# Attention scores on halves of the array's rows, norm rows loaded later, six further weight slots

## The chip, the cores and the metric

The kernel runs on one core of a Trainium2 chip. Such a core has a matrix engine (PE, TensorE), a vector engine (DVE), an activation engine (ACT), GpSimd (POOL), a queue engine (SP) that here issues the weight loads, and 16 DMA engines that all queues share. The metric is the device time of one execution in microseconds (us). 0.5% of it is 6.5 us.

## What is computed

Two layers over 256 tokens of width 1024. Layer 0 mixes by attention, layer 1 by a Hyena convolution; each is followed by a layer norm, a mixture of experts (16 experts, two per token) and a second layer norm. Only layer 0's attention and the very last layer norm are touched:

```python
def diff_attention(q, k, v, lam):            # 4 heads x 2 maps of width 64, q: 256 rows, k: 512
        s = jnp.einsum('bqhmd,bkhmd->mbhqk', q_blk, k).astype(jnp.float32) * scale
        p = jax.nn.softmax(s, axis=-1)
        a = (p[0] - lam * p[1]).astype(v.dtype)

def window_gqa_latent(q, k, v, k_ctx, v_ctx, sink):   # 8 query heads of width 64, 2 key heads
    s_loc = jnp.einsum('bnqhgd,bnkhd->bnhgqk', qb, kb).astype(jnp.float32) * scale
    s_ctx = jnp.einsum('bnqhgd,bchd->bnhgqc', qb, k_ctx).astype(jnp.float32) * scale

    for i in range(DEPTH):
        ...
        x = layer_norm(DEEPNORM_ALPHA * x + g1 * y, ln_g[i, 0], ln_b[i, 0])
        f = moe_ffn(x * (1 + sc2) + sh2, router_w, router_bias, exp_w_gate[i], exp_w_up[i], exp_w_down[i])
        x = layer_norm(DEEPNORM_ALPHA * x + g2 * f, ln_g[i, 1], ln_b[i, 1])
```

## The kernel before

**Weights.** All weights come in loads of 1 MB on SP's queue (`load`, L144), each into a slot of 8 KB per partition. There is a ring of 12 slots, and in the expert part of layer l there are MORE[l] further slots, w0, w1, ..., through which the ring then turns too (`all_slots`). A load waits until the instructions that read the slot's last content are done, and SP takes its loads strictly in order. A transfer is thus started by the engine that frees a slot, nearly always PE.

**Attention (layer 0).** `proj` makes the projections (L937), and a `fin_` function each finishes them per 128 tokens: rope on DVE, transposes on PE into a bank of PSUM, an evacuation by ACT (`evac`, L162). A head is 64 wide, the array has 128 rows. fin_q therefore writes each query head into a tile zq with a block of 64 zeros (memset by POOL) in the middle, and transposes it twice, shifted by 64, so that qaZ and qwZ hold the transposed query of one head on one half of the rows and zeros on the other. A score (diff_scores L1004, win_scores L1033) is then one matmul over all 128 rows, 128 queries by 512 keys, against both heads' keys; two of them (m = 0, 1) make a unit, each followed by its maximum on DVE (L1005, L1035). `interleave` writes units, their outputs (L1021, L1060) and the further projections and modulation vectors (DVE L269; their sums on PE, L281, in column strips of 32) among one another. A scheduler at build time sets each engine's order from that.

**Experts.** A layer has ten places p. Each place loads an expert's 12 MB (four pairs of gate and up, four down), multiplies the gathered tokens (`up` L646, `down` L665, `back` L684, DVE L690), and places 1 to 8 also carry a piece of a dense treatment of the two fullest experts: odd ones `dense_up` (L709, four loads), even ones `dense_down` (L721, two loads). At p == 9 (NEST) there are first MORE[l] loads of the tenth expert into the further slots, then the `back` of the ninth, then `rare`: a nest of conditional branches (L759) for cases that these inputs don't have, which every engine passes by itself without doing anything; and behind it the remaining 12 − MORE[l] loads into the ring and the tenth expert's work. One place earlier, `all_slots(0)` takes the further slots out of the ring.

**End.** The last layer norm's factors (gbf, 1 MB for all 128 partitions) are loaded by POOL right after the first layer's end (L1399), into a pool of their own. L359 to L365 make the statistics, L1407 and L1408 the rows, and four transfers store them.

## Time and profile before

| | us |
|---|---|
| median of three runs | 1301.54 (1300.76 to 1306.81) |
| the profiled execution | 1297.5 |
| its span, first to last instruction | 1295.7 |
| PE busy | 1161.9 (90%) |
| DVE busy | 549.3 (42%) |
| ACT busy | 214.9 (17%) |

All rows come from the profiled execution; its times count from the span's start. A row of the timeline joins instructions of one kind: start, duration, engine, line, operands, and the number of records in it. Matrix products in f32 leave two records each. A busy PE says that matmuls overlap without a gap, not how fast they are: the start of the next row tells more than the duration of one. A row of the waits names the engine and line that waited, what it waited for, the time in all, how often, and the longest. "SPq", "PEq" are the queues of SP and PE: the time in which an engine handles its branches and semaphores.

### The profile page before, as it was taken

How to read it: one execution, taken by the hardware profiler on the slowest of the kernel's cores; microseconds unless marked ns; L12 is line 12 of the kernel's file. 1: busy time of each engine (PE TensorE's matmuls, PEld its weight loads, DVE VectorE, ACT ScalarE, POOL GpSimd, SP SyncE). 2: the span in 40 equal slices, each digit the busy share in tenths (PEclk: the TensorE clock that was granted, in tenths of full speed). 3: DMA queues.
4: the chain of work that ended last, by engine and by line, in shares of the span. 5: the costliest groups of instructions: out<-in, count | busy, mean ns of one | idle time of the engine just before them, and what ended most of it. 6: DMA issues, size and time to landing. Idle time of an engine off the chain costs nothing. (4 is left out here: it accounts for less than half of the span.)

```text
span 1295.7 us, 19951 instructions
## 1 busy us (share of the span) xinstructions
PE 1161.9 (90%) x8106; PEld 696.2 (54%) x8106; DVE 549.3 (42%) x1131; ACT 214.9 (17%) x431; POOL 48.8 (4%) x88
## 2 busy tenths in 40 slices
PE   5999989979999989999686779899699999999983
PEld 2345645448437466485443468684374374665741
DVE  2376998461231432414311268993712213223133
ACT  2133646120000000000000044410300000000000
POOL 1000000210000000000200010000100000000000
PEclk9999999989999999999778789999899999999986
DMA  9999894879998998999999784378799999999964
GB/s 325 397 402 349 307 356 180 310 263 406 409 401 340 400 401 329 397 398 363 382 385 395 294 345 177 109 299 316 266 405 408 402 358 396 405 373 401 408 249 196
DMA packets 133206, 443.87 MB, mean 343 GB/s; under 512 B 8271, under 2 KB 9895, under 8 KB 133104
## 3 DMA queue, kind: packets, MB, share of 16 engines
q1 hardware_dynamic: 127168, 426.76, 85.0%
q0 software_dynamic: 4864, 13.18, 3.0%
q10 hardware_dynamic: 1072, 2.54, 0.6%
q8 instruction: 67, 1.10, 0.3%
q14 instruction: 35, 0.29, 0.1%
HBM read 437.19 MB, written 5.26 MB: 341 GB/s over the span
## 5 line engine op out<-in xcount | busy, mean ns | idle before, releaser
L646 PE MATMUL acc<-w,xe 128*32 128x256 f32 (+1 forms) x2688 | 217.6, 430 | 11.4 <-PEq L759 5.9
L709 PE MATMUL acc<-xnT,w 128*128 128x256 f32 x1024 | 222.3, 379 | 0.0
L709 PEld LDWEIGHTS acc<-xnT,w 128*128 128x128 f32 x1024 | 194.4, 190 | 25.6
L646 PEld LDWEIGHTS acc<-w,xe 128*32 128x32 f32 (+1 forms) x2688 | 102.4, 120 | 115.0 <-issue 66.6
L665 PE MATMUL acc<-w,aT 128*32 128x256 f32 (+1 forms) x1344 | 115.5, 420 | 10.2 <-DMA w<-in_exp_w_down 6.0
L721 PE MATMUL acc<-w,hid 128*128 128x512 f32 x256 | 111.4, 593 | 0.3 <-DVE xs L690 0.3
L712 DVE TENSOR_TENSOR hid<-hid,acc 128x256 f32<-128x256 f32 x32 | 13.5, 421 | 197.0 <-ACT hid L711 197.0
L665 PEld LDWEIGHTS acc<-w,aT 128*32 128x32 f32 (+1 forms) x1344 | 47.5, 116 | 63.6 <-issue 27.4
L269 DVE SCALAR_TENSOR_TENSOR w<-w,cz 128x1024 f32<-128x1024 f32 x60 | 75.8, 1289 | 11.4 <-DMA w<-in_mod_w 11.4
L721 PEld LDWEIGHTS acc<-w,hid 128*128 128x128 f32 x256 | 48.1, 190 | 58.1 <-issue 57.3
L690 DVE TENSOR_TENSOR xs<-xs,acc 128x512 f32<-128x512 f32 x92 | 57.4, 682 | 47.5 <-PE acc L684 47.5
L937 PE MATMUL acc<-w,hT 128*128 128x512 f32 (+1 forms) x192 | 71.2, 523 | 0.0
L650 DVE TENSOR_TENSOR ac<-ac,acc 128x256 f32<-128x256 f32 (+1 forms) x23 | 10.7, 467 | 138.3 <-PE acc L646 138.3
L1294 PE MATMUL acc<-hTh,w 128*128 128x256 f32 x320 | 59.9, 286 | 0.0
L723 DVE SCALAR_TENSOR_TENSOR do<-acc,wtP,g2b 128x512 f32<-128x512 f32 x32 | 24.0, 751 | 69.6 <-PE acc L721 69.6
L937 PEld LDWEIGHTS acc<-w,hT 128*128 128x128 f32 x192 | 35.6, 190 | 31.7 <-issue 29.3
L1294 PEld LDWEIGHTS acc<-hTh,w 128*128 128x128 f32 x320 | 49.6, 188 | 2.2 <-ACT ed L1324 1.3
L711 ACT ACTIVATE hid<-acc 128x256 f32<-128x256 f32 x32 | 12.3, 383 | 207.7 <-PE acc L709 207.7
L649 ACT ACTIVATE ac<-acc 128x256 f32<-128x256 f32 (+1 forms) x23 | 9.7, 420 | 217.0 <-PE acc L646 217.0
L614 PE MATMUL mis<-h,Pu 128*32 128x256 f32 (+1 forms) x336 | 33.6, 462 | 13.3 <-DVE Pu L608 8.5
L1294 PE MATMUL acc<-hTl,w 128*128 128x256 f32 x160 | 44.8, 280 | 0.0
L684 PE MATMUL acc<-xg,PT 32*128 32x256 f32 (+1 forms) x336 | 39.9, 441 | 4.1 <-DVE xg L670 3.8
(351 smaller groups left out, 1264.9 us busy)
## 6 DMA issues: line engine op xcount, KB each, us to landing
w<-in_exp_w_gate SPq DMA_DIRECT2D x108, 1024.0 KB, 17.5
w<-in_exp_w_up SPq DMA_DIRECT2D x108, 1024.0 KB, 17.4
w<-in_exp_w_down SPq DMA_DIRECT2D x108, 1024.0 KB, 14.2
w<-in_mod_w SPq DMA_DIRECT2D x40, 1024.0 KB, 9.0
w<-in_hy_w_in SPq DMA_DIRECT2D x12, 1024.0 KB, 19.5
w<-in_attn_w_in SPq DMA_DIRECT2D x9, 1024.0 KB, 11.2
w<-in_mod_w SPq DMA_DIRECT2D x16, 512.0 KB, 10.8
w<-in_attn_w_out SPq DMA_DIRECT2D x4, 1024.0 KB, 11.7
```

The costliest lines, as they stand in the source:

```text
L269: dve.scalar_tensor_tensor(out=st["acc"][:, k], in0=w[:, k], scalar=c_[k], in1=st["acc"][:, k], op0=ALU.mult, op1=ALU.add)
L614: pe.matmul(gb[S * j:S * j + S, 0:nn], Pu[:, t, 0:S], self.h2[:, t, nn * j:nn * j + nn], start=(t == 0), stop=(t == 1), tile_position=(0, ...
L646: pe.matmul(A[m][S * j:S * j + S, 0:nn], self.xe[:, kc, :], w[:, nn * j:nn * j + nn], tile_position=(0, S * j), start=(kc == 0), stop=(kc ...
L665: pe.matmul(y[S * q:S * q + S, 0:nn], lhs, w[:, nn * q:nn * q + nn], tile_position=(0, S * q), start=(kc == 0), stop=(kc == KC - 1))
L684: pe.matmul(o, self.PT[r, 128 * t:128 * t + 128], self.yb[r, 0:nn], start=True, stop=True, tile_position=(S * q, 0))
L690: dve.tensor_tensor(out=x_, in0=x_, in1=o, op=ALU.add)
L709: pe.matmul(b[:, N * m:N * m + N], ws[m][kc // 4][:, kc % 4, 128 * fb:128 * fb + 128], h2T[:, kc, :], start=(kc == 0), stop=(kc == KC - 1))
L712: dve.tensor_tensor(out=hid[:, fb, :], in0=hid[:, fb, :], in1=b[:, N:2 * N], op=ALU.mult)
L721: pe.matmul(b, hid[:, fb, 128 * t:128 * t + 128], ws[fb // 2][:, fb % 2, s_], start=(fb == 0), stop=(fb == 3))
L723: dve.scalar_tensor_tensor(out=o, in0=b, scalar=wt[:, t], in1=g2b[:, s_], op0=ALU.mult, op1=ALU.mult)
L937: pe.matmul(bank[:, 0:width], hT[:, kc, 128 * t:128 * t + 128], st["w"][kc // per][:, kc % per, :], start=(kc == 0), stop=(kc == KC - 1))
L1294: pe.matmul(b[:, 0:N], w_, m, start=(kc == 0 and i == 0), stop=(kc == KC - 1 and i == len(ps) - 1))
```

## The change

Three edits. First, query heads are no longer padded. qaT and qwT hold two heads on the two halves of the rows; fin_q makes 4 transposes and one evacuation instead of 8 and 2, without zq and the memset. Each score multiplies 64 rows only, with a tile position (0 or 64) that names the half. For the window heads, each of the two key heads must then stand on both halves: fin_kw copies it twice on ACT (L1005 of the new file) and makes two transposes per 128 tokens instead of one. In a unit both matmuls are written ahead of the two maxima.

Second, gbf and its pool are gone. `norm_rows` loads the same rows on POOL's queue after `rare` in the expert part of layer 1, into tiles "hid" and "do" of the dense pieces, and `moe` itself calls `store`.

Third, MORE[1] is 6 instead of 5: with 18 slots the sixth load of the tenth expert goes ahead of the nest, and six instead of seven follow it.

The diff, with context and the removed copy of `store` cut:

```diff
@@ -26,7 +26,7 @@
 PAD = -3e38
 RING = 12
 
-MORE = [4, 5]
+MORE = [4, 6]
 
 
 DENSE = 2
@@ -725,7 +725,29 @@
 
         ENG = [ET.PE, ET.Activation, ET.DVE, ET.Pool, ET.SP]
 
-        def moe(l, h2, R, first, filler):
+        def store(gf, bf):
+
+            ov = O["out"].rearrange("o (t p) d -> p (o t) d", p=128)
+            st = [ln_stats(xs[:, t, :], 1) for t in range(2)]
+            for t in range(2):
+                mv, rs = st[t]
+                for hf in range(2):
+                    s_ = slice(512 * hf, 512 * hf + 512)
+                    dve.scalar_tensor_tensor(out=xs[:, t, s_], in0=xs[:, t, s_], scalar=mv[:, 0:1], in1=gf[:, s_], op0=ALU.subtract, op1=ALU.mult)
+                    dve.scalar_tensor_tensor(out=xs[:, t, s_], in0=xs[:, t, s_], scalar=rs, in1=bf[hf], op0=ALU.mult, op1=ALU.add)
+                    if t:
+                        (act if hf else sp).dma_start(out=ov[:, t, s_], in_=xs[:, t, s_])
+                if t == 0:
+                    sp.dma_start(out=ov[:, t, :], in_=xs[:, t, :])
+
+        def norm_rows(mp, l, i):
+            g = row_bc(mp, I["ln_g"][l, i:i + 1, :], "hid", pool)
+            b = [mp.tile([128, 512], F32, name="do", tag="do", bufs=2) for _ in range(2)]
+            for hf in range(2):
+                pool.dma_start(out=b[hf], in_=I["ln_b"][l, i:i + 1, 512 * hf:512 * hf + 512].to_broadcast([128, 512]))
+            return g, b
+
+        def moe(l, h2, R, first, filler, fin=None):
             with tc.tile_pool(name=f"mp{l}", bufs=2, reuse_waits="tile") as mp:
...
@@ -744,10 +766,7 @@
-                lng = row_bc(mp, I["ln_g"][l, 0:1, :], "hid", pool)
-                lnb = [mp.tile([128, 512], F32, name="do", tag="do", bufs=2) for _ in range(2)]
-                for hf in range(2):
-                    pool.dma_start(out=lnb[hf], in_=I["ln_b"][l, 0:1, 512 * hf:512 * hf + 512].to_broadcast([128, 512]))
+                lng, lnb = norm_rows(mp, l, 0)
...
@@ -808,6 +827,8 @@
                         last.back()
                         last = None
                         rare(RARE)
+                        if fin:
+                            rows = norm_rows(mp, l, 1)
                         E.bank = E.banks()
                         E.w = expert_loads(l, ix, have=w)
@@ -852,6 +873,8 @@
                 last.back()
 
                 act.activation(dumm, epsc[:, 0:1], AF.Sqrt)
+                if fin:
+                    fin(*rows)
...
@@ -875,7 +898,7 @@
         with tc.tile_pool(name="s0", bufs=1) as s0:
 
             hT = s0.tile([128, KC, 512], F32, name="hT0")
-            qaZ = s0.tile([128, 8, N], F32, name="qaZ")
+            qaT = s0.tile([128, 4, N], F32, name="qaT")
             kaT = s0.tile([128, 4, 512], F32, name="kaT")
...
@@ -901,8 +924,8 @@
-            qwZ = s0.tile([128, 8, N], F32, name="qwZ")
-            kwT = s0.tile([128, 512], F32, name="kwT")
+            qwT = s0.tile([128, 4, N], F32, name="qwT")
+            kwT = s0.tile([128, 2, 512], F32, name="kwT")
...
@@ -951,23 +974,19 @@
-            def fin_q(dst, pair):
-
+            def fin_q(dst):
 
                 def fin(t, bank):
-                    o = s0.tile([128, 4, 3, 64], F32, name="zq", tag="zq")
-                    pool.memset(o[:, :, 1, :], 0.0)
-                    do_rope(o[:, :, 0::2, :], pair(bank), t, 8)
-                    for half in range(2):
-                        tb = mbank()
-                        for b in range(4):
-                            src = o[:, b].rearrange("p c d -> p (c d)")[:, 64 * half:64 * half + 128]
-                            pe.transpose(tb[:, 128 * b:128 * b + 128], src, ident)
-                        evac(dst(half)[:, :, 128 * t:128 * t + 128], tb.rearrange("p (a b) -> p a b", a=4), "a")
+                    o = tmp()
+                    v4 = lambda x_: x_.rearrange("p (h m d) -> p h m d", d=64, m=2)
+                    do_rope(v4(o), v4(bank), t, 8)
+                    tb = mbank()
+                    for b in range(4):
+                        pe.transpose(tb[:, 128 * b:128 * b + 128], o[:, 128 * b:128 * b + 128], ident)
+                    evac(dst[:, :, 128 * t:128 * t + 128], tb.rearrange("p (a b) -> p a b", a=4), "a")
                 return fin
 
-            fin_qa = fin_q(lambda m: qaZ[:, m::2, :], lambda b: b.rearrange("p (h m d) -> p h m d", d=64, m=2))
-            fin_qw = fin_q(lambda g: qwZ[:, 4 * g:4 * g + 4, :], lambda b: b.rearrange("p (g j d) -> p j g d", d=64, g=2))
+            fin_qa, fin_qw = fin_q(qaT), fin_q(qwT)
 
...
@@ -979,9 +998,13 @@
                     do_rope(v4(o), v4(bank[:, 0:128]), t, 2)
                 else:
                     evac(o, bank[:, 0:128], "a")
+
                 tb = mbank()
-                pe.transpose(tb[:, 0:128], o, ident)
-                evac(kwT[:, 128 * t:128 * t + 128], tb[:, 0:128], "a")
+                for g in range(2):
+                    o2 = tmp()[:, 0:128].rearrange("p (a d) -> p a d", a=2)
+                    act.activation(o2, o[:, None, 64 * g:64 * g + 64].to_broadcast([128, 2, 64]), AF.Copy)
+                    pe.transpose(tb[:, 128 * g:128 * g + 128], o2.rearrange("p a d -> p (a d)"), ident)
+                evac(kwT[:, :, 128 * t:128 * t + 128], tb[:, 0:256].rearrange("p (a b) -> p a b", a=2), "a")
                 evac(vw[:, t, :], bank[:, 128:256], "a")
 
             SC = 0.125
@@ -1001,7 +1024,9 @@
                 bk = [abank(), abank()]
                 pt = [tmp(), tmp()]
                 for m in range(2):
-                    pe.matmul(bk[m], qaZ[:, 2 * h + m, 128 * qc:128 * qc + 128], kaT[:, h, :], start=True, stop=True)
+                    r = slice(64 * m, 64 * m + 64)
+                    pe.matmul(bk[m], qaT[r, h, 128 * qc:128 * qc + 128], kaT[r, h, :], start=True, stop=True, tile_position=(64 * m, 0))
+                for m in range(2):
                     dve.tensor_reduce(out=mx[:, m:m + 1], in_=bk[m], axis=AX.X, op=ALU.max)
@@ -1030,7 +1055,9 @@
                 pt = [tmp(), tmp()]
                 oc = 128 * (1 - qc)
                 for m in range(2):
-                    pe.matmul(bk[m], qwZ[:, 2 * hp_ + m, 128 * qc:128 * qc + 128], kwT, start=True, stop=False)
+                    r = slice(64 * m, 64 * m + 64)
+                    pe.matmul(bk[m], qwT[r, hp_, 128 * qc:128 * qc + 128], kwT[r, hp_ // 2, :], start=True, stop=False, tile_position=(64 * m, 0))
+                for m in range(2):
                     pe.matmul(bk[m][:, oc:oc + 128], id_bf, mask_bf[qc], start=False, stop=True)
                     dve.tensor_reduce(out=mx[:, m:m + 1], in_=bk[m], axis=AX.X, op=ALU.max)
                 sk2 = sink[:, 2 * hp_:2 * hp_ + 2]
@@ -1393,23 +1420,7 @@
-        gp = es.enter_context(tc.tile_pool(name="gp", bufs=1, reuse_waits="tile", side="right"))
-        gbf = gp.tile([128, 2, D], F32, name="gbf")
-        for a, nm in enumerate(("ln_g", "ln_b")):
-            pool.dma_start(out=gbf[:, a], in_=I[nm][1, 1:2, :].to_broadcast([128, D]))
-        moe(1, h2, R, first, None)
...
+        moe(1, h2, R, first, None, store)
         less_ring(rmore)
 
 
```

What the build makes of it on the engines:

PE in the attention, from the fourth score on. L1004 is the score before, L983 the transpose of fin_kw, L937 a projection, L993 a transpose of probabilities. Before:

```order
L1004 MATMUL acc4_624<-kaT_114,qaZ_113 128x512
L1004 MATMUL acc5_625<-kaT_114,qaZ_113 128x512
L983 MATMUL mis0_614<-blob_72,tmp_608 128x128
L281 MATMUL acc0_647<-w_516,one_f_77 32x512 x2
L937 MATMUL acc1_650<-w_597,hT0_112 128x256 x8
L1004 MATMUL acc2_671<-kaT_114,qaZ_113 128x512
L1004 MATMUL acc3_672<-kaT_114,qaZ_113 128x512
L993 MATMUL mis0_686<-blob_72,tmp_584 128x128 x4
L1004 MATMUL acc4_714<-kaT_114,qaZ_113 128x512
```

After (the score is L1028, the kw transpose L1006, the projection L960, the transpose of probabilities L1016):

```order
L1028 MATMUL acc4_615<-kaT_114,qaT_113 128x512
L1028 MATMUL acc5_616<-kaT_114,qaT_113 128x512
L281 MATMUL acc0_638<-w_502,one_f_77 32x512 x2
L960 MATMUL acc1_641<-w_583,hT0_112 128x256 x2
L1006 MATMUL mis0_600<-blob_72,tmp_601 128x128
L1006 MATMUL mis0_600<-blob_72,tmp_604 128x128
L960 MATMUL acc1_641<-w_583,hT0_112 128x256 x6
L1028 MATMUL acc2_667<-kaT_114,qaT_113 128x512
L1028 MATMUL acc3_668<-kaT_114,qaT_113 128x512
L1016 MATMUL mis0_682<-blob_72,tmp_570 128x128 x4
L1028 MATMUL acc4_710<-kaT_114,qaT_113 128x512
```

Some pairs of scores stand next to each other in both, others have transposes between them; the kw transposes are two and stand within the projection.

SP ahead of the nest of layer 1: the end of the ninth expert's loads, and the early loads of the tenth. A name w followed by a number and an underscore is a further slot, w_ is the ring. Before:

```order
L144 DMA w3_8590<-in_exp_w_gate 128x2x1024
...
L144 DMA w4_8592<-in_exp_w_up 128x2x1024
...
L144 DMA w_8594<-in_exp_w_gate 128x2x1024
...
L144 DMA w_8596<-in_exp_w_up 128x2x1024
...
L144 DMA w_8608<-in_exp_w_down 128x2x1024
...
L144 DMA w_8610<-in_exp_w_down 128x2x1024
...
L144 DMA w_8618<-in_exp_w_down 128x2x1024
...
L144 DMA w0_8806<-in_exp_w_gate 128x2x1024
...
L144 DMA w1_8808<-in_exp_w_up 128x2x1024
...
L144 DMA w4_8814<-in_exp_w_gate 128x2x1024
...
L759 COMPARE_AND_BRANCH
```

After:

```order
L144 DMA w_8580<-in_exp_w_gate 128x2x1024
...
L144 DMA w_8582<-in_exp_w_up 128x2x1024
...
L144 DMA w0_8594<-in_exp_w_down 128x2x1024
...
L144 DMA w1_8596<-in_exp_w_down 128x2x1024
...
L144 DMA w_8598<-in_exp_w_down 128x2x1024
...
L144 DMA w_8604<-in_exp_w_down 128x2x1024
...
L144 DMA w0_8792<-in_exp_w_gate 128x2x1024
...
L144 DMA w1_8794<-in_exp_w_up 128x2x1024
...
L144 DMA w2_8796<-in_exp_w_gate 128x2x1024
...
L144 DMA w5_8802<-in_exp_w_up 128x2x1024
...
L778 COMPARE_AND_BRANCH
```

Left out are instructions that make addresses, and loads of the same kind. The further slots held gate and up weights of the ninth expert before; now w0 and w1 hold the two loads of its dense down piece, ahead of the same slots' loads for the tenth expert.

PE at the end of that dense down piece. Before:

```order
L721 MATMUL acc4_8432<-w_8608,hid_8456 128x512 x2
L721 MATMUL acc4_8432<-w_8610,hid_8456 128x512 x2
L721 MATMUL acc5_8433<-w_8608,hid_8456 128x512 x2
L721 MATMUL acc5_8433<-w_8610,hid_8456 128x512 x2
L665 MATMUL acc2_8430<-w_8612,aT_8719 32x256 x8
```

After:

```order
L721 MATMUL acc4_8418<-w0_8594,hid_8442 128x512 x2
L721 MATMUL acc4_8418<-w1_8596,hid_8442 128x512 x2
L721 MATMUL acc5_8419<-w0_8594,hid_8442 128x512 x2
L721 MATMUL acc5_8419<-w1_8596,hid_8442 128x512 x2
L665 MATMUL acc2_8416<-w_8598,aT_8705 32x256 x8
```

The order is the same, and what is read is now w0 and w1 (the two names of the weights), each by eight calls, the last ones right ahead of the ninth expert's down projection (L665).

## Rows read from the trace of the kernel before

**Rows 1.** Chain that ended last, its one long piece: start us, us, what.

```profile
1260.62 17.64 DMA w<-in_exp_w_down
```

**Rows 2.** SP timeline, loads around the nest: start, us, queue, line, operation.

```profile
1231.65 0.37 SPq L144 DMA_DIRECT2D w<-in_exp_w_gate  x1
1256.60 0.39 SPq L144 DMA_DIRECT2D w<-in_exp_w_up  x1
...
1258.92 2.08 SPq L144 DMA_DIRECT2D w<-in_exp_w_down  x4
```

**Rows 3.** SP waits in 1231 to 1262: total us, times, longest.

```profile
SPq L759 <- SPq L759: 14.5, 4, 5.2
SPq L144 <- PEq L759: 8.7, 1, 8.7
```

**Rows 4.** Nest branch L759 on SP: ns min/median/max, first and last start us.

```profile
L759 SPq EVENT_SEMAPHORE  x18: 17/17/17, 703.3 to 1247.6; - x18
L759 SPq COMPARE_BRANCH  x6: 34/44/58, 595.5 to 1232.7; - x6
```

**Rows 5.** PE timeline, the last dense down projection ahead of the nest.

```profile
1234.20 13.90 PE L721 MATMUL acc<-w,hid 128*128 128x512 f32 x32
```

**Rows 6.** Windows at the nest: length, busy by engine, PEclk, DMA share, GB/s.

```profile
1247.00:1253.00 6.00, 5.45 (x81) 2.89 (x81) 1.87 (x3) 0.00 (x0) 0.00 (x0) 1.00 0.00 0
1259.00:1274.00 15.00, 11.10 (x138) 5.36 (x134) 0.42 (x1) 2.05 (x3) 0.00 (x0) 0.73 1.03 413
```

**Rows 7.** SP waits at the nest of layer 0, in 697.4 to 722.

```profile
SPq L759 <- SPq L759: 15.1, 2, 9.8
```

**Rows 8.** Window of SP's passage in layer 0.

```profile
698.00:714.00 16.00, 11.48 (x158) 5.37 (x153) 0.42 (x1) 0.77 (x2) 0.00 (x0) 0.82 0.87 347
```

**Rows 9.** Windows over the attention.

```profile
65.00:115.00 50.00, 50.00 (x141) 22.30 (x138) 31.88 (x32) 14.80 (x20) 0.62 (x2) 1.00 0.97 374
115.00:165.00 50.00, 50.00 (x209) 30.52 (x209) 46.85 (x91) 26.98 (x60) 1.03 (x2) 1.00 0.89 332
165.00:200.00 35.00, 27.84 (x130) 15.02 (x129) 32.82 (x64) 18.94 (x36) 2.94 (x4) 1.00 0.78 300
200.00:247.00 47.00, 47.00 (x278) 25.32 (x277) 30.44 (x78) 18.57 (x49) 6.30 (x11) 1.00 0.67 250
```

**Rows 10.** DVE waits in 100 to 116.

```profile
DVE mr L164 <- PE acc L281: 11.5, 1, 11.5
```

**Rows 11.** PE timeline in the attention: start, us, line, operands, shapes, records.

```profile
129.40 0.27 PE L983 MATMUL mis<-blob,tmp 128*128 128x128 f32 x1
129.51 1.02 PE L1004 MATMUL acc<-kaT,qaZ 128*128 128x512 f32 x2
130.46 1.05 PE L281 MATMUL acc<-w,one_f 128*32 128x512 f32 x4
131.45 1.98 PE L1004 MATMUL acc<-kaT,qaZ 128*128 128x512 f32 x4
133.27 1.05 PE L1021 MATMUL mis<-va,tmp 128*128 128x128 f32 x8
```

**Rows 12.** PE timeline, back step of a 64-row expert, and what follows.

```profile
1080.21 1.99 PE L684 MATMUL acc<-xg,PT 64*128 64x512 f32 x8
1082.13 0.44 PE L655 MATMUL acc<-blob,ac 128*128 128x128 f32 x2
```

**Rows 13.** ACT groups in 75 to 190: count, busy us, mean ns, idle before.

```profile
L162 ACT ACTIVATE qaZ<-mis 128x512 f32<-128x512 f32 x4 | 2.2, 594 | 13.1 <-PE mis L965 13.1
...
L162 ACT ACTIVATE kwT<-mis 128x128 f32<-128x128 f32 x4 | 1.1, 277 | 2.6 <-PE mis L983 2.6
```

**Rows 14.** Windows in the expert nests of layer 0 and layer 1.

```profile
404.00:416.00 12.00, 12.00 (x67) 8.73 (x65) 2.08 (x7) 1.15 (x3) 0.00 (x0) 1.00 0.62 232
940.00:1231.00 291.00, 284.57 (x2086) 177.95 (x2082) 67.45 (x137) 15.73 (x38) 0.00 (x0) 1.00 1.01 395
```

**Rows 15.** Waits in 744 to 800, at the start of the Hyena.

```profile
ACT hT L383 <- DMA w<-in_hy_w_in: 2.3, 1, 2.3
```

More of the change, by code (lines that the diff above doesn't have):

```diff
@@ L1395, in emit @@
                 h2, first = mixer_tail(1, s1b, z2T, wo, R)
-        gp = es.enter_context(tc.tile_pool(name="gp", bufs=1, reuse_waits="tile", side="right"))
-        gbf = gp.tile([128, 2, D], F32, name="gbf")
-        for a, nm in enumerate(("ln_g", "ln_b")):
-            pool.dma_start(out=gbf[:, a], in_=I[nm][1, 1:2, :].to_broadcast([128, D]))
-        moe(1, h2, R, first, None)
-        ov = O["out"].rearrange("o (t p) d -> p (o t) d", p=128)
-        st = [ln_stats(xs[:, t, :], 1) for t in range(2)]
-        for t in range(2):
-            mv, rs = st[t]
-            for hf in range(2):
-                s_ = slice(512 * hf, 512 * hf + 512)
-                dve.scalar_tensor_tensor(out=xs[:, t, s_], in0=xs[:, t, s_], scalar=mv[:, 0:1], in1=gbf[:, 0, s_], op0=ALU.subtract, op1=ALU.mult)
-                dve.scalar_tensor_tensor(out=xs[:, t, s_], in0=xs[:, t, s_], scalar=rs, in1=gbf[:, 1, s_], op0=ALU.mult, op1=ALU.add)
-                if t:
-                    (act if hf else sp).dma_start(out=ov[:, t, s_], in_=xs[:, t, s_])
-            if t == 0:
-                sp.dma_start(out=ov[:, t, :], in_=xs[:, t, :])
+        moe(1, h2, R, first, None, store)
         less_ring(rmore)
```

## The prediction

> **What bounds the kernel now.** I read four views, and each is needed because no single engine is the limit from end to end. The **chain of waits** is short: it holds only the last 39 us. In it, look at the one long piece, the last 1 MB load of expert weights, which lands at 1260.62 + 17.64 = 1278.26; what follows (down projection, expansion, normalization, store) runs 17.4 us to the end of the span at 1295.7 [rows 1]. So the end is the landing of that load plus a fixed tail. The **SP queue's timeline and waits** say why it lands then. Before the nest SP issues its last early load at 1231.65; the next is issued at 1256.60, and the four loads after it of the down projection from 1258.92 [rows 2]. Between them SP waits 14.5 us for itself in the four branches of the skipped nest and then 8.7 us for PE [rows 3]: its last compare stands at 1232.7, its last event of the nest at 1247.6 [rows 4]. SP's own passage takes 1247.6 − 1232.7 = 14.9 us, and today it costs nothing, because PE (dense down projection, back, its own branch) is later still. The DMA engines are idle meanwhile (0 GB/s in 1247 to 1253) and saturated at 413 GB/s after it, 2.54 us for 1 MB [rows 6].
>
> Further ahead, the **windows** give the reason why time saved early reaches the end: PE has no gap at 404 to 416 while the DMA is at 0.62, and is busy 284.57 of 291 us in the expert nest of layer 1 [rows 14], so loads are issued as PE frees slots, and a PE that is earlier moves them. For the attention, PE is full in 65 to 165 and 200 to 247; in 165 to 200 it is DVE (32.82 of 35 us) [rows 9]. At 114 it is PE alone: DVE waits 11.5 us there for it [rows 10].
>
> **Part 1, scores on half the rows.** A full 128x512 call costs 1.82 / 2 = 0.91 us (1.82 from the start of two at 131.45 to what follows at 133.27) [rows 11]. The trace has no score on half the rows. The nearest row is the "back" step of a 64-row expert: four calls of 64x512, in pairs on the two halves, from 1080.21 to 1082.13, so 0.96 a pair [rows 12]. A second one is L281: two calls in different column strips take 0.99 together, from 130.46 to 131.45 [rows 11]. A pair of scores that stand next to each other would thus cost 0.96 and not 1.82: 0.86 less. But only adjacent pairs gain. In the new PE order 7 of the 16 pairs are adjacent (4 of the 8 diff pairs, 3 of the 8 window pairs); the other 9 have transposes, weight projections or masks between, and a single half-row call streams the same 512 columns. Gain 7 x 0.86 = 6.0 us. Transposes: fin_q has 4 instead of 8 in each of its 4 calls, 16 x 0.11 = 1.8 us less (0.11 from 129.40 to 129.51) [rows 11]; fin_kw has 4 more, 0.4. The 18 separate calls and the pairs switch the array's tiling; L281 shows what that costs, 0.99 − 0.91 = 0.08 for both sides, 18 x 0.08 = 1.4 us. PE's sum: −6.0 − 1.8 + 0.4 + 1.4 = −6.0 us; without any price of switching −7.4.
>
> How much of it passes on, stretch by stretch: ahead of 114, fin_qa's 8 transposes, 0.9 us, all of it, since DVE waits for PE there. In 115 to 165, 4 pairs (3.4) less the kw transposes (0.4) and 8 separate calls (0.6): 2.4; DVE is busy 46.85 of 50 and so could follow 3.1 at most; I take 2.0. In 165 to 200 DVE is the bound, its instructions are the same, and I take 0. In 200 to 231, two adjacent pairs less six separate calls, 1.7 − 0.5 = 1.2, with DVE half idle (30.44 of 47). Sum −4.1 us; ends 0 (DVE holds everything, or switching costs more) and −7.4. ACT's edits go together: 4 evacuations of 594 ns fall away, 8 copies like the 277 ns one of kwT come, a swap at −2.4 + 2.2 us [rows 13]; ACT is idle 23 of 50 us in 115 to 165 and hides it; were it not hidden, its end would still be under 1 us. The four memsets of POOL hold nobody.
>
> **Part 2, the normalization's rows leave the start of the Hyena.** 1 MB less at 747, where the only wait for a load is ACT's for hy_w_in, 2.3 us [rows 15], whose successor then waits for DVE. I take −0.2; ends 0 and −2.3. The rows are loaded again behind the nest on POOL's queue, beside the last six loads of SP; their tiles wait for PE and DVE to pass the nest. They are needed only by the normalization, after the last load.
>
> **Part 3, six further slots: here the sum turns.** The sixth load, 2.54 us, goes ahead of the nest, so one less follows it: −2.5 us. But 18 slots instead of 17 turn the ring by other steps. In the old order the slots w0 to w4 hold gate and up weights of the last expert ahead of the nest, free by 1231. In the new order **w0 and w1 hold the two loads of the dense down projection**, and L721 reads both up to its last matmuls: it loops over output halves and token tiles outside, weights inside. The new w0 can be issued after L721's 14th of 16 calls, w1 after the 16th, at 1234.20 + 13.90 = 1248.1 [rows 5]. SP takes its queue in order, so w2 to w5 (free long since) stand behind them, and behind these the branch. w1 to w5 at some 0.65 us each (three loads from 1256.60 to 1258.92, 0.77 each, and the four behind them 2.08, 0.52 each [rows 2]): w5 at about 1250.7, the compare 1.05 us later as today (1231.65 to 1232.7), 1251.8; plus 14.9 us of passage, 1266.7, and the first load behind the nest at about 1267.0 instead of 1256.60. That is 10.4 us later, with one load less: **+7.9 us**. The cover is gone: SP's passage had 8.7 us of slack, and it starts 19 us later.
>
> Ends of this term. Lower: the passage is hidden by other means, and only the DMA holds: today 7 loads take 1278.26 − 1256.60 = 21.66 us from the first issue; 12 loads and 1 MB of rows from 1246.4 take 21.66 + 6 x 2.54 = 36.9, landing at 1283.3, +5.0. Upper: the passage has run only with the DMA half idle here; of its four parts the longest, 5.2 us [rows 3], lies in the stretch with traffic. Four of that length would be 20.8 instead of 14.5, +6.3, so +14.2. In layer 0, where the DMA moved 347 GB/s during it, two parts took 15.1 us [rows 7, 8]; that is nearest, so I keep 14.9 as the value.
>
> **Sum.** Profiled execution 1297.5 us (span 1295.7 and 1.8 around it): −4.1 − 0.2 + 7.9 = +3.6, so 1301.1. The median of the three runs is 1301.54, 4.0 above the profiled one; there it is **1305.1 us**.
>
> **Rivals.**
> *SP's passage grows under traffic* (the slower side). w0 to w5 and the rows now stream through the whole passage, where today it is half idle. For it: 5.2 us for the first part, in traffic, against (14.5 − 5.2) / 3 = 3.1 for each of the others, and a part of 9.8 in layer 0 [rows 3, 7]. Against: layer 0's passage, under traffic for most of it, is no longer than layer 1's. At the upper end, −4.3 + 14.2 = +9.9: 1311.4. It decides from a passage of 18 us on, 3 us above today's, where the whole comes to over +6.5.
>
> *The scores gain nothing*: pairs run one after the other, or DVE holds the attention throughout. Then −0.2 + 7.9 = +7.7: 1309.2. For it: DVE is at 94% in 115 to 200; against: L684's and L281's pairs overlap. The same time comes out if entering and leaving the half-row tiling costs more than seen in L281: 7 pairs and 18 calls switch 50 times, and 7.4 / 50 = 0.15 us each eats the gain. The Trainium skill, "TensorEngine Tiling (Array Packing)", Key Properties, speaks for this: "Mode switching requires drain: Changing tiling mode (not just tile) drains the TensorE". By that rule each switch has a price, which the trace bears out only as far as L281's 0.08 us for two.
>
> *The six loads are not held* (w0 and w1 come free earlier, or the change does in the end only what it says). They would fill the idle window of the DMA; rows and six loads are then as many bytes as seven loads today, the tail is level or 2.6 us better if the rows land in the window: −4.3 to −6.9, 1294.6 to 1297.2. Against: the reads of w0 and w1 by L721 are in the order itself.
>
> *The attention gives all of it*, −7.4: about +0.3, 1301.8.
>
> **Chances.** Forecast, with both terms near their values (+1 to +6.4): 0.52. Passage grows: 0.16. No gain in the scores: 0.15. Loads not held: 0.10. Full gain in the scores: 0.07. A measurement of this kernel can tell 0.5%, 6.5 us, from no change: slower than 1308.0 are the second case, two thirds of the third and a little of the first, 0.28; faster than 1295.0 are four in ten of the fourth, 0.04; the rest, 0.68, is within. The range leaves out the case of the loads that are not held and the upper end of the passage, and holds the rest: 1299 to 1311.
>
> **What would show it.** In the profile after: (a) L1028 in pairs of 4 records in about 1 us where they stand together; qa's first DVE wait ends about 1 us earlier and the dense part ahead of the nest about 4. (b) SP issues w0 only when L721 is in its last calls, and the five others within 4 us; no DMA traffic for some 14 us before that. (c) SP's wait for PE at the nest is gone, the first load behind the nest comes some 20 us after w0's, and the last down load lands about 7.9 − 4.3 = 3.6 us later than 1278.3. (d) The rows land before the last load. The prediction is wrong if SP issues the six while the dense part is still at its beginning, or if its passage is over before PE's.

## The result and the profile after

The changed kernel took 1315.11 us (median) against 1301.15 for the kernel before on the same chip, a ratio of 1.0105 with a 95% interval of 1.0082 to 1.0129: **14.0 us slower**, where 3.6 were forecast. It lies above the upper end of the range, 1311, and above every rival. The profiled execution of after is one of 1315.11 us (span 1313.3), 17.6 us longer than the profiled one of before, which lay 3.6 below the median of its kernel here (1297.5). Differences of milestones below come from these two executions and hold the 3.6 us between 17.6 and 14.0 somewhere; in layer 0's experts one execution differs from another of the same work by up to 4 us, so I read places there no closer than that.

Where the time came in, by the start of the same step in the two traces:

| step | before | after | later by |
|---|---|---|---|
| first score | 114.08 | 113.55 | −0.5 |
| L281 at the end of the stretch to 170 | 168.64 | 169.70 | +1.1 |
| output projection of layer 0 | 215.37 | 222.19 | +6.8 |
| first `up` of layer 1 | 922.27 | 930.05 | +7.8 |
| L721 ahead of the nest | 1234.20 | 1241.94 | +7.7 |
| last `down` (L665) | 1278.31 | 1294.91 | +16.6 |
| end of the span | 1295.7 | 1313.3 | +17.6 |

So there are two costs: some 7 us by the end of the attention (6.8 at the output projection, 7.7 at L721), passed on whole through both layers, and 8.9 us at the nest. The last 1.0 us is the same final steps at a lower granted clock (0.54 in 1294 to 1300, 0.78 in 1278 to 1284 before).

**The nest.** The chain of waits after has the same long piece as [rows 1], 18.4 us later (start, us, what); L665 waits for its landing at 1294.87:

```profile
1279.06 15.81 DMA w<-in_exp_w_down
1294.87 0.04 issue
1294.91 1.98 PE acc L665 x16
```

The SP timeline after, early loads and first loads behind the nest, to be held against [rows 2]:

```profile
1254.15 0.37 SPq L144 DMA_DIRECT2D w<-in_exp_w_gate  x1
1255.87 0.37 SPq L144 DMA_DIRECT2D w<-in_exp_w_up  x1
...
1258.15 0.37 SPq L144 DMA_DIRECT2D w<-in_exp_w_up  x1
1275.95 0.38 SPq L144 DMA_DIRECT2D w<-in_exp_w_gate  x1
```

SP's waits after in 1230 to 1300 (who, for whom: total us, times, longest), for [rows 3]:

```profile
SPq L144 <- PE acc L721: 23.8, 2, 22.7
SPq L778 <- SPq L778: 16.1, 5, 5.0
```

The instructions of the nest's branch line on SP after (ns min/median/max, first and last start us), for [rows 4]:

```profile
L778 SPq EVENT_SEMAPHORE  x18: 17/17/17, 711.9 to 1275.6; - x18
L778 SPq COMPARE_BRANCH  x6: 34/46/58, 603.6 to 1259.2; - x6
```

The dense down piece of after on PE, for [rows 5], and a window in its middle (columns as in [rows 6]):

```profile
1241.94 13.90 PE L721 MATMUL acc<-w,hid 128*128 128x512 f32 x32
```

```profile
1244.00:1247.00 3.00, 3.00 (x8) 1.33 (x7) 0.00 (x0) 0.00 (x0) 0.00 (x0) 1.00 0.00 0
```

SP's wait for PE at the nest is gone. In its place SP stands 22.7 us on L721 for w0, which is issued 12.2 us into L721's 13.9, w1 at L721's end; during that the DMA engines move nothing. Then follow SP's passage, from 1259.2 to 1275.6, 16.4 us, and the first load behind the nest, 34.0 us after the start of L721 where it was 22.4. The last load lands 18.9 us after that one (21.66 before, with seven loads): 34.0 − 22.4 = 11.6 later, 2.7 given back, 8.9.

**The attention.** A window of before that [rows 9] has only as part of longer ones (length, busy of PE, PEld, DVE, ACT and POOL, PEclk, DMA share, GB/s):

```profile
185.00:205.00 20.00, 17.76 (x89) 9.50 (x87) 18.83 (x51) 17.10 (x38) 1.60 (x2) 1.00 0.49 187
```

The same window of after, and a short one ahead of it, at the first pair of window scores:

```profile
175.00:178.00 3.00, 3.00 (x10) 1.27 (x9) 3.00 (x5) 0.94 (x1) 0.00 (x0) 0.50 1.02 421
```

```profile
185.00:205.00 20.00, 15.21 (x45) 7.25 (x45) 16.17 (x39) 11.64 (x25) 1.60 (x2) 0.59 0.52 184
```

**The granted clock has fallen to 0.59** in 185 to 205, and PE executes half as many matmuls there, 45 records for 89. PE's timeline after shows the two costs (columns as in [rows 11]). First, what a half-row call costs at the full clock:

```profile
113.55 1.12 PE L1028 MATMUL acc<-kaT,qaT 64*128 64x512 f32 x2
114.61 0.66 PE L295 MATMUL mis<-blob,mr 128*128 128x128 f32 x4
...
119.91 1.13 PE L1028 MATMUL acc<-kaT,qaT 64*128 64x512 f32 x4
120.97 1.05 PE L281 MATMUL acc<-w,one_f 128*32 128x512 f32 x4
...
127.13 0.66 PE L1016 MATMUL mis<-blob,tmp 128*128 128x128 f32 x4
127.72 1.12 PE L1028 MATMUL acc<-kaT,qaT 64*128 64x512 f32 x2
...
133.23 0.60 PE L1016 MATMUL mis<-blob,tmp 128*128 128x128 f32 x4
133.66 1.68 PE L960 MATMUL acc<-w,hT 128*128 128x256 f32 x7
```

An adjacent pair takes 120.97 − 119.91 = 1.06 us (1.71 to 1.82 before), a single half-row call 1.06 too (0.86 to 0.96 for a single full one; 0.95 from 129.51 to 130.46 in [rows 11]). The neighbours pay as well: four transposes take 0.59 between two half-row calls, and 0.43 between full-row work at 133.23. Second, the same calls in 191 to 205, where each takes about twice that:

```profile
191.57 2.07 PE L1059 MATMUL acc<-kwT,qwT 64*128 64x512 f32 x2 [4.79 <-DVE mr L164]
193.57 1.97 PE L1157 MATMUL mis<-blob,o_sb 128*128 128x128 f32 x8
...
202.85 2.08 PE L1059 MATMUL acc<-kwT,qwT 64*128 64x512 f32 x4
204.86 1.47 PE L1087 MATMUL mis<-tmp,vw 128*64 128x128 f32 x16
```

2.0 us from a half-row call's start to the next row, against 1.05: that is the lower of the clock's two levels, 1.2 GHz. There is also a new wait of 4.79 us ahead of it. Either could be cause or consequence, which the experiments had to tell apart. The trace itself shows that the clock first fell at the window scores near 175, for some 3 us, before that wait.

### The profile page after: what moved, and what is told of

Same layout as the page of the kernel before. It is cut to its first block, busy times and chain, and to the rows that moved or that the text cites. A ratio compares the mean times of both kernels' runs of the same rounds, so it can differ in the third digit from the quotient of the medians.

```text
span 1313.3 us, 19930 instructions
## 1 busy us (share of the span) xinstructions
PE 1170.4 (89%) x8094; PEld 695.4 (53%) x8094; DVE 549.5 (42%) x1131; ACT 215.1 (16%) x435; POOL 48.7 (4%) x85
## 5 line engine op out<-in xcount | busy, mean ns | idle before, releaser
L665 PE MATMUL acc<-w,aT 128*32 128x256 f32 (+1 forms) x1344 | 115.3, 420 | 8.3 <-DMA w<-in_exp_w_down 4.1
L721 PE MATMUL acc<-w,hid 128*128 128x512 f32 x256 | 111.4, 593 | 0.3 <-DVE xs L690 0.3
L665 PEld LDWEIGHTS acc<-w,aT 128*32 128x32 f32 (+1 forms) x1344 | 47.6, 116 | 61.5 <-issue 27.3
L721 PEld LDWEIGHTS acc<-w,hid 128*128 128x128 f32 x256 | 48.0, 190 | 58.2 <-issue 57.2
L960 PE MATMUL acc<-w,hT 128*128 128x512 f32 (+1 forms) x192 | 71.8, 523 | 0.0
L960 PEld LDWEIGHTS acc<-w,hT 128*128 128x128 f32 x192 | 35.4, 190 | 31.8 <-issue 29.7
## 6 DMA issues: line engine op xcount, KB each, us to landing
w<-in_mod_w SPq DMA_DIRECT2D x16, 512.0 KB, 10.8
```

The lines of the kernel that those rows point to most:

```text
L665: pe.matmul(y[S * q:S * q + S, 0:nn], lhs, w[:, nn * q:nn * q + nn], tile_position=(0, S * q), start=(kc == 0), stop=(kc == KC - 1))
L721: pe.matmul(b, hid[:, fb, 128 * t:128 * t + 128], ws[fb // 2][:, fb % 2, s_], start=(fb == 0), stop=(fb == 3))
L960: pe.matmul(bank[:, 0:width], hT[:, kc, 128 * t:128 * t + 128], st["w"][kc // per][:, kc % per, :], start=(kc == 0), stop=(kc == KC - 1))
```

## The experiments: the nest

**The tail alone**: the kernel before with the normalization's rows moved and six further slots, its attention untouched.

```diff
-MORE = [4, 5]
+MORE = [4, 6]
...
                         rare(RARE)
+                        if fin:
+                            rows = norm_rows(mp, l, 1)
...
```

> The kernel before with the attention untouched, and the other two edits: the rows of the last norm loaded behind the nest, and six further slots. Theory A (the loss has two separate parts, attention and tail): the attention ends as before, dense down of the ninth place starts within 1 us of 1234, and the end is 9 to 10 us later than before, ratio about 1.007. Theory B (the late weights only follow from the attention being late): no loss, ratio 0.998 to 1.000.

Measured: 1309.96 us, ratio 1.0062 (1.0040 to 1.0084), +8.2 by medians. The first `up` of layer 1 is 0.8 later than before, the last landing 10.9. SP's timeline:

```profile
1247.18 0.38 SPq L144 DMA_DIRECT2D w<-in_exp_w_gate  x1
...
1270.12 0.39 SPq L144 DMA_DIRECT2D w<-in_exp_w_gate  x1
```

With L721 at 1234.96, w0 comes 12.2 us into it, as in after. The passage takes 17.6 us here, from 1252.2 to 1269.8. So the slots and rows cost some 8 us without any help of the attention.

**Five slots**: the changed kernel with `MORE = [4, 5]`.

> The changed kernel with five further slots instead of six in layer 1, everything else as changed. The slots turn as in the kernel before, so the dense down piece of the ninth place is in ring slots. Theory A (the six slots cost 9 us at the end, because w0 and w1 hold the dense down piece): SP issues its five early loads during the ups of the ninth expert, waits for PE at the nest again, and the whole is about 8 to 10 us faster than the changed kernel, some 5 to 7 us slower than the kernel before. Theory B (the end is late because of the rows' 1 MB on POOL's queue behind the nest): the tail stays 8 to 10 us long and the time is that of the changed kernel within 2 us.

Measured: 1310.8 us, ratio 1.0068 (1.0045 to 1.0091). The early loads go out from 1235.07 and are all issued by 1242.5, so nothing is held by L721 any more. The first load behind the nest is at 1267.47, 10.9 later than before, and L721 starts 10.8 later, so the nest itself adds nothing. Yet the kernel is 9.1 us slower than before, where 5 to 7 were expected. Its chain of waits holds, as the last landing,

```profile
1271.45 20.71 DMA w<-in_exp_w_down
```

and the last load lands 24.7 us after the first one behind the nest, 3.0 more than the 21.66 of before, with the same seven loads: the 1 MB of rows on POOL's queue goes beside them. So the moved rows have a price of their own, which the six slots hide in after, since there they stream during SP's long passage.

**The further slots leave the ring earlier**: the tail alone, with `all_slots(0)` ahead of the dense loads of the ninth place, so that w0 and w1 no longer hold dense weights.

```diff
+                        if p + 1 == NEST:
+                            all_slots(0)
                         if p in PIECES:
...
-                        if p + 1 == NEST:
-                            all_slots(0)
```

> The kernel before with the attention untouched, rows behind the nest and six slots as changed, and one thing else: the further slots leave the ring before the dense loads of the ninth place instead of behind them, so that the dense down piece lies in ring slots and w0 to w5 are free early. Theory A (w0 and w1 hold SP): SP issues all six early loads between 1222 and 1232, passes the nest ahead of PE as in the kernel before, its first load behind the nest stands within 1 us of 1256.6, and the tail loses only what the rows' 1 MB costs beside the last loads: one load less (2.5 us) against 3.6 us for the rows (the run with five slots lost 3.6 us between dense down and the last down projection), so 1 us slower to 1 us faster than before. Theory D (the nest's passage itself got longer by six loads): as long as with the slots held, ratio 1.006.

Measured: 1302.42 us, ratio 0.9992 (0.9973 to 1.0012). The six early loads go out from 1231.41 to 1240.26; L721 runs from 1240.00, so they no longer wait for its end. The last landing, from the chain of waits,

```profile
1266.00 18.77 DMA w<-in_exp_w_down
```

stands 44.8 us behind the start of L721, 0.7 more than before. The one moved line takes back 7.5 of the 8.2 us; what holds w0 is thus shown. The places themselves are not where they were expected: the first load behind the nest is at 1262.45, 5.9 us later than before, because L721 starts 5.8 later in this execution, 3.3 of it by the output projection, with an attention that is that of before. The section on the attention comes back to this.

**And the rows behind the last loads**: the kernel of the last experiment, with the rows issued by SP after the tenth expert's last down load.

```diff
                         rare(RARE)
-                        if fin:
-                            rows = norm_rows(mp, l, 1)
                         E.bank = E.banks()
                         E.w = expert_loads(l, ix, have=w)
+                        if fin:
+                            rows = norm_rows(mp, l, 1, sp)
```

> As the run before it, and the rows of the last norm are issued by SP behind the last down load instead of by POOL beside the six. They land some 2.5 us after that load and are needed about 8 us after it. Theory A: the rows cost nothing any more, the sixth early load is all gain, the last down load lands 2.5 us earlier than before relative to the dense down piece: 2 to 3 us faster than the kernel before, ratio 0.998. Theory E (the last load is bound by something else than bytes, such as its order on the queue): no gain, ratio 1.000 or above.

Measured: 1299.01 us, ratio 0.9968 (0.9951 to 0.9986), 2.9 us faster than before. The end of SP's loads, and the last landing in the chain of waits:

```profile
1259.88 0.39 SPq L144 DMA_DIRECT2D w<-in_exp_w_gate  x1
...
1263.97 0.37 SPq L350 DMA_DIRECT2D hid<-in_ln_g  x1
```

```profile
1263.42 15.69 DMA w<-in_exp_w_down
```

The six loads land 19.2 us after the first (1279.11 − 1259.88), against 22.3 in the experiment ahead of it, where the rows ran beside them. Against the start of L721 the last landing is 2.6 us earlier than before. This is the gain that the sixth slot was to bring, 2.5 us, once neither L721 nor the rows stand in its way.

## The experiments: the attention

**Half rows alone, same order**: the kernel before with its padded tiles, where each score multiplies only the 64 rows that aren't zero. Nothing else differs, not even the order of PE.

```diff
-  pe.matmul(bk[m], qaZ[:, 2 * h + m, ...], kaT[:, h, :], ...)
+  pe.matmul(bk[m], qaZ[64*m:64*m+64, 2 * h + m, ...], kaT[64*m:64*m+64, h, :], ..., tile_position=(64*m, 0))
-  pe.matmul(bk[m], qwZ[:, 2 * hp_ + m, ...], kwT, ...)
+  pe.matmul(bk[m], qwZ[64*g:64*g+64, 2 * hp_ + m, ...], kwT[64*g:64*g+64], ..., tile_position=(64*g, 0))   # g = hp_ // 2
```

> The kernel before, where only the score matmuls take half the rows, out of the same padded tiles: 64 rows with a tile position, the order of all engines as before, transposes, evacuations and loops too. For the window heads both of a pair lie on the same half, so only diff pairs that are adjacent can run together. Theory A (the attention is lost by an order in which PE waits, and the clock falls after that wait): PE has no wait over 2 us in 165 to 215, the granted clock stays 1.0 there, and what is left is 4 adjacent pairs less (4 x 0.76 = 3.0 us) and 24 separate calls with some 0.15 to 0.3 us of switching each (3.6 to 7.2): the output projection starts 0 to 4 us later than 215.4. Theory B (half-row matmuls lower the granted clock): it is 0.5 to 0.8 in part of 165 to 210 here too, and the output projection starts 6 to 8 us later.

Measured: 1321.14 us, ratio 1.0153 (1.0127 to 1.0179), the slowest of all. Its windows:

```profile
185.00:205.00 20.00, 20.00 (x41) 8.08 (x41) 11.50 (x31) 12.01 (x23) 1.04 (x1) 0.50 0.30 115
205.00:225.00 20.00, 19.75 (x70) 10.64 (x70) 8.62 (x22) 6.99 (x20) 0.56 (x1) 0.50 0.15 53
```

PE has no gap in 185 to 205 and yet stands at 0.50 throughout; the same windows of before have 1.00. A score takes 2.0 us there and 1.05 again after the clock's return at 225:

```profile
185.82 2.07 PE L1034 MATMUL acc<-kwT,qwZ 64*128 64x512 f32 x2
187.82 2.07 PE L1021 MATMUL mis<-va,tmp 128*128 128x128 f32 x8
...
225.11 1.12 PE L1034 MATMUL acc<-kwT,qwZ 64*128 64x512 f32 x2
226.16 0.66 PE L993 MATMUL mis<-blob,tmp 128*128 128x128 f32 x4
```

No PE wait ahead of it is longer than 1.6 us, and before has these waits too, at the full clock. The output projection starts 18.7 us later than before. The half-row calls are the only difference, and the clock is low for 40 us.

**The new order of the loops alone**: full rows, padded, with both matmuls of a unit ahead of the two maxima, as in the change.

> The kernel before, with full padded rows, where only the loops of a score unit are split so that both matmuls are written ahead of the two maxima. In the order of PE the second score of the second window unit then stands ahead of the third unit, as in the changed kernel, and waits for the bank that holds modulation sums. Theory A (the order makes the wait): PE waits 3 to 5 us for DVE's copy of these sums, the granted clock falls to 0.5 for some us behind it, and the output projection starts 3 to 7 us later than 215.4, ratio 1.002 to 1.005. Theory B (half rows): no such wait and no lower clock, within 1 us of the kernel before.

Measured: 1303.14 us, ratio 1.0009 (0.9994 to 1.0023). Its window, and PE's longest wait in 165 to 225:

```profile
185.00:205.00 20.00, 16.84 (x95) 9.74 (x96) 18.43 (x52) 16.62 (x37) 1.60 (x2) 1.00 0.49 189
```

```profile
PE mis L1132 <- DVE mx L1040: 3.1, 1, 3.1
```

PE is idle for more of it than in before, has a wait of 3.1 us, and keeps the full clock; after's 4.8 us is longer, and a wait of that length with full rows was not tried.

But full rows don't always keep the full clock. The tail alone (first line) and the run in which the further slots leave the ring earlier (second and third) have the attention of before, and in them it dips:

```profile
185.00:205.00 20.00, 17.76 (x83) 9.92 (x82) 17.26 (x47) 16.10 (x35) 1.60 (x2) 0.91 0.46 183
```

```profile
165.00:185.00 20.00, 15.33 (x63) 7.60 (x62) 17.13 (x25) 4.85 (x7) 1.35 (x2) 0.91 1.00 388
185.00:205.00 20.00, 17.50 (x83) 10.07 (x83) 17.39 (x45) 15.77 (x34) 1.60 (x2) 0.91 0.49 172
```

Ahead of these dips stand waits of at most 1.6 us and short calls, as in before, where the clock stays full. Their output projections start 1.8 and 3.3 us later than that of before. So a dip to 0.91 in 20 us, after's 0.91 in 165 to 185 included, is no sign of half rows; 0.5 to 0.74 is.

**Which of the two parts**: half rows out of padded tiles, in the differential scores only, and (a single execution) in the window scores only.

> The kernel before, where only the diff scores take half the rows (same padded tiles, same order); the window scores keep all 128 rows. Theory B, sharpened (half-row scores lower the granted clock where nothing dense stands between them, in the window scores from 170 to 225; the diff scores lie among full projections): the granted clock stays 1.0 to 247, and the time is that of the kernel before within 2 us (in the run with both, the stretch from 113.5 to 169.8 was 0.3 us shorter). Theory C (the diff scores start it and the window scores only suffer): the clock falls here too in 183 to 225, and 10 us or more are lost.

> The counterpart: only the window scores take half the rows, in the old order, and both of a pair lie on the same half. Theory B: the granted clock is 0.5 from about 184 to 224 and the output projection starts 17 to 20 us later than 215.4. Theory C: the clock stays 1.0 and the output projection starts within 3 us of 215.4.

Measured: the differential scores alone 1301.87 us, ratio 0.9996 (0.9978 to 1.0014); the window scores alone 1314.43 us, with the output projection 1.3 and 12.2 us later than before. The window 185 to 205 of the first, then 185 to 225 of the second:

```profile
185.00:205.00 20.00, 17.75 (x84) 9.90 (x83) 17.25 (x47) 15.95 (x34) 1.59 (x2) 0.93 0.45 171
```

```profile
185.00:205.00 20.00, 18.94 (x60) 9.05 (x60) 15.89 (x42) 13.72 (x29) 1.60 (x2) 0.74 0.45 165
205.00:225.00 20.00, 20.00 (x87) 10.40 (x87) 10.15 (x29) 7.93 (x23) 0.00 (x0) 0.66 0.04 7
```

The clock is low for long with the window scores. The 0.93 of the differential ones is no more than the dips with full rows; it comes over 30 us after the last half-row call, and nothing shows that it comes from them. 17 to 20 us of delay were expected of the window part; less came.

The stretch from the L281 near 169 to the output projection tells the two groups of kernels apart, one execution of each: 45.2 to 50.0 us in the seven of this document whose window scores take all rows, 51.1 to 65.8 in the five with half-row ones in about the same order.

**Adjacent pairs**: the changed attention, with the score matmuls given precedence at build time (`with tc.high_priority(offset=2000):`), so that 7 of the 8 window pairs stand adjacent instead of 3. The nest is the mended one with the rows last. The question was whether an empty half of the array lowers the clock, or the half-row calls as such.

> The changed attention as it is, with the mended tail of the run with the rows last, and one more edit: the score matmuls are given precedence at build time, so that in PE's order 7 of the 8 window pairs stand next to each other (3 in the changed kernel) and can run on both halves at once. Theory F (the clock falls because separate half-row calls leave half of the array empty): with the pairs together the granted clock stays at 0.9 or above in each 20 us from 165 to 247, and the output projection starts within 3 us of 215.4. Theory G (half-row calls lower the clock in this stretch however they stand, or the order makes PE wait): 0.5 to 0.8 in part of it again and the output projection 6 us or more later.

Measured: 1302.27 us, ratio 1.0002 (0.9986 to 1.0018), where the mended nest alone gave 0.9968. The output projection is 7.3 us later than before.

```profile
185.00:205.00 20.00, 16.73 (x56) 8.58 (x55) 17.46 (x40) 12.21 (x26) 1.21 (x3) 0.66 0.56 223
```

The clock still falls, without a PE wait over 1.1 us, so after's wait of 4.8 us isn't needed for it. Standing adjacent did not put most pairs on both halves at once, however:

```profile
188.26 1.26 PE L1061 MATMUL acc<-kwT,qwT 64*128 64x512 f32 x4 [0.69 <-ACT qwT L162]
...
204.14 1.79 PE L1061 MATMUL acc<-kwT,qwT 64*128 64x512 f32 x4
205.86 0.66 PE L1016 MATMUL mis<-blob,tmp 128*128 128x128 f32 x4
```

From the pair at 204.14 to the next row it is 1.72 us, where a pair that runs together takes 1.06. Of the seven adjacent pairs three start together, the others' calls 0.5 to 0.7 us apart. One of the three, at 188.26, stands right where the clock falls. So an empty half isn't needed at that point; that it plays no part at all is not shown. The precedence also moves the first differential scores from 113 to 88 us and projections behind them, so the 7.3 us aren't those of the window pairs alone.

## The experiments: both together

**The changed kernel with the mended nest** (a single execution).

> The changed kernel with the mended tail (further slots out of the ring one step earlier, rows issued by SP behind the last load): what is left of the loss is the attention's. If attention and tail are separate and add up: dense down starts 7 to 10 us later than in the kernel before, the tail behind it is 2.5 us shorter, 1306 to 1309 us.

Measured: 1304.03 us, a little better than expected, 2.6 above the kernel before on that chip. The first `up` of layer 1 is 8.9 us later than before, the last landing 6.9. With the 2.9 that the mended nest gains, the attention alone costs 2.6 + 2.9 = 5.5 us by medians; the tail alone costs 8.2; together 13.7 of the 14.0 measured. The 2.6 come from one execution, and the 17 of the kernel before on that chip lie between 1295.9 and 1305.2, so the sum is closer than it had to be.

**What is worth keeping**: differential queries unpadded and scored on half rows, window scores padded over full rows as before, the mended nest with six slots and the rows last.

> Mended tail with the rows last, and of the attention's edit only the diff half: query heads of the diff part unpadded (4 transposes and one evacuation instead of 8 and 2 in two calls), their scores on half the rows; the window part as in the kernel before, padded, on all rows. In PE's order 7 of the 8 diff pairs are adjacent, as it falls out. By the pieces measured: 8 transposes less (0.9 us), pairs together for 7 x 0.76 us less their switching, which took back most of it in the two runs with diff halves; DVE bounds 165 to 200. So the output projection starts 0 to 2 us earlier than 215.4 if the clock holds, and the whole is 2 to 5 us faster than before, ratio 0.996 to 0.9985. If diff halves alone lower the clock later on, 2 us or more later and a ratio of 0.999 or above.

Measured: 1293.16 us, ratio **0.9940** (0.9918 to 0.9962), 8.3 us faster than before, where 2 to 5 were expected, and faster than every other kernel here. The output projection starts 3.8 us earlier than before. Its windows:

```profile
165.00:185.00 20.00, 17.10 (x84) 10.18 (x83) 18.59 (x31) 7.82 (x12) 2.29 (x3) 0.91 1.02 400
185.00:205.00 20.00, 17.38 (x100) 9.97 (x100) 18.98 (x53) 15.39 (x39) 0.96 (x2) 1.00 0.33 128
```

In 185 to 205 the clock is full, where after has 0.59; the 0.91 ahead of it is a dip as with full rows. 2.9 us are the nest's; how the rest divides between pairs, transposes and the order isn't separated.

## Why the prediction was wrong

**Part 3, the nest, was right in its mechanism and nearly in its size.** Shifted by the 7.7 us with which L721 starts, the forecast issue of w0 was 1254.1 and of w1 1255.8; measured 1254.15 and 1255.87. w5 was due at 1258.4 and came at 1258.15. The passage was put at 14.9 and took 16.4 (17.6 in the tail alone), so that term became 11.6 instead of 10.4; the load less gave 2.7 instead of 2.5. The sum is +8.9 where +7.9 was forecast. The rival in which the passage grows was thus right in direction, but stayed under the 18 us from which it was to decide. PE's passage grew as well, its longest part to 6.0 us, without ending last. Of the signs, (a) came only in the pairs' 1.06 us; (b), (c) up to its last clause, and (d) came as described: the rows, issued at 1267.0 to 1268.1, land within 8 us, ahead of the last load.

**Part 1 failed, in the step "How much of it passes on".** It forecast −4.1 us; the attention costs some 5.5 by medians, and that is nearly the whole gap between 3.6 and 14.0. The step had four stretches, and their durations were all taken at the clock of the kernel before:

- Ahead of 114, −0.9 forecast, −0.5 measured.
- 115 to 165, −2.0 forecast. From 113.55 to the L281 at 169.70 the stretch is 56.15 us, before 54.56: +1.6. The scores themselves, start to start, take 12.47 instead of 14.23: about 2.8 less in the four adjacent pairs (3.4 taken), 1.1 more in the eight single calls. Everything around them takes 3.35 more. 0.87 of it are the kw transposes, 1.41 instead of 0.54 (0.4 taken). 1.40 come from the new order, which the sum had left out: kw transposes part two L281 calls that ran together before (139.47, first below, then the rows of after), 0.98 + 0.97 instead of 0.99, and four transposes of probabilities, 0.44, now stand ahead of 169.70. The 1.08 left over are with the neighbours of half-row calls. So the price of switching, 0.6 in the sum, came to about 1.1 + 1.1 = 2.2.

```profile
139.47 1.05 PE L281 MATMUL acc<-w,one_f 128*32 128x512 f32 x4
```

```profile
138.54 1.05 PE L281 MATMUL acc<-w,one_f 128*32 128x512 f32 x2
139.52 0.44 PE L1006 MATMUL mis<-blob,tmp 128*128 128x128 f32 x2
139.89 1.04 PE L281 MATMUL acc<-w,one_f 128*32 128x512 f32 x2
```

- 165 to 200, 0 forecast, and 200 to 231, −1.2 forecast. From the L281 to the output projection, 46.73 us became 52.49: **+5.8**, with the clock at 0.59 in 20 us of it and PE's wait of 4.8 us. No rival had it. This is the term that failed: a lower clock was put at nothing. What the wait adds of its own isn't separated; with the adjacent pairs, where it is gone, the clock still falls. Nor are the 5.8 us exact, since the same stretch differs by up to 3.2 between executions with the attention of before. The prediction read PEclk 1.00 in every row of [rows 9] and took it as a property of the place, though the change alters the very calls that PE makes there.

The Trainium skill, "TensorEngine Tiling (Array Packing)", Key Properties, says that a change of tiling mode drains the engine. By that rule every switch has a price, and the rows agree: 2.2 us in after for twelve places with a half-row call or pair, 0.09 us a side by this estimate. In the padded kernel, whose order is that of before, the pairs take 2.7 us less (4.37 instead of 7.06) and the stretch only 0.1 less (54.45), so that 2.6 went to switching, 0.11 a side. The rival that named the page put 0.15 a switch as the point at which the gain is eaten, and up to 170 the gain was eaten indeed; the rest of the 1.6 us is the kw transposes and the order.

An adjacent pair gained 0.65 to 0.76 for itself where 0.86 was taken. The best kernel, whose diff pairs are adjacent in 7 of 8 cases, starts the output projection 3.8 us earlier.

**Part 2** was taken as −0.2 and can't be seen in a spread of 3 us. That the rows compete with the last loads was left out of the sum on the ground that they land earlier; that holds with six held slots, and costs 3 us as soon as the slots are not held.

**What stays open.** Half-row window scores hold the granted clock low for far longer than full rows do, shown by the padded kernel, whose order is that of before. Why is not shown. In 165 to 225 the clock falls close behind waits of PE, or in one, in every trace in which it falls; with full rows it is back after some 3 us. Why it stays low with the window scores is only argued: between them stand mostly short calls, between the differential ones projections over all 128 rows. Nor is it settled what of a half-row call matters, its rows, its tile position or the switches around it. Why the padded kernel stayed low for some 40 us and the changed one for 15 to 20 wasn't tried either.

## What to carry to other kernels

Changing a ring's length moves every later load to another slot: see which slots the in-order queue will then meet first, and who still reads them; here one misplaced release stood ahead of twelve loads. Small data that is needed last goes behind the critical transfers on the same queue, not beside them on another. Matmuls on part of the array save time where two run next to each other, as between the projections here; look at the granted clock of the stretch after the change, for a busy PE does not show its loss.

## What was not expected of the hardware

- The granted clock fell to 0.50, the 1.2 GHz level, with PE busy for 20.00 of 20 us, when the f32 scores used 64 of 128 rows; with full rows in the same order it was 1.00, and 0.91 in two other executions. The output projection came 18.7 us later.
- A wait of 3.1 us on PE, with full rows, left the clock at 1.00; behind waits of at most 1.6 us it dipped to 0.91 in 20 us in two other executions with full rows.
- A half-row f32 call of 64x512 took 1.06 us alone and 1.06 us as a pair, a full-row call alone 0.86 to 0.96; four transposes took 0.16 us more between two of them.
- Two L281 calls in different column strips took 0.99 us together, and 1.95 when two transposes stood between them.
- SP's way through the skipped nest took 14.9 us before, 16.4 after and 17.6 with the tail alone.
